# Recurrent mixer of a three-block layer stack: products on the two halves of the array's rows issued in turns

## The chip, the core and the metric

The kernel runs on one core of one Trainium2 chip. A core has a matrix engine (TensorE; PE in the profile, its weight loads PEld), a vector engine (DVE), a scalar engine (ACT), GpSimd (POOL) and a queue that issues transfers (SP). The matrix engine writes into PSUM, which has eight banks of 512 float32 numbers on each of 128 partitions. The metric is the device time of one execution in microseconds; lower is better.

## What is computed

Three transformer-like blocks run one after another on 1024 tokens of 1024 channels, all in float32. Only the second one matters here; of it, the recurrent group (eight heads of 64 channels). In short:

```python
def second_block(x, ...):
    h = rmsnorm(x, norm_mix_g[l])
    p = h @ w_in[l]
    p_rwkv = token_shift_mix(p[..., :D_RWKV_IN])
    y_rwkv = rwkv7_group(p_rwkv, ...)          # a state of 64x64 per head, carried over the tokens
    y_conv = conformer_conv_group(p[..., D_RWKV_IN:], ...)
    x = x + jnp.concatenate([y_rwkv, y_conv], axis=-1) @ w_out[l]
    ...                                         # feed-forward, norm
```

`rwkv7_group` updates a state per head at every token (a decay, a rank-one correction along a normalized key, and a new key-value product) and reads it with the receptance. The kernel computes it chunk by chunk: within a chunk of 64 tokens by products of matrices, from chunk to chunk by the state.

## The kernel before

The first and the third block, and the second block's projections and feed-forward, are long rows of matrix products from one helper (line 251). Between the second block's projections and its output projection stands the stage that the change touches: `rwkv`, lines 1242 to 1602.

It works on eight blocks of 128 tokens, two chunks of 64 in each, all eight heads at a time. A chunk's keys and directions lie on one half of the 128 partitions or the other, in such a way that what belongs to chunk 0 of a block and what belongs to chunk 1 meet on opposite halves. Many products therefore contract over 64 partitions alone (the upper or the lower half of the array's rows). For each block five generators run side by side, each on another block: `rwkv_prep` (the chunk's operands and their products within the chunk), `rwkv_solve` (small triangular inverses, on DVE and by transfers), `rwkv_pre` (what does not wait for the state), `rwkv_chain` (the state's way) and `rwkv_out` (norm and gate). `rwkv` puts them into rounds: in one round block i is in the chain, i + 1 in pre, i + 2 in solve, i + 3 in prep, i - 1 in out.

The six groups of products of 64 rows are these. For each the first operand is the half's weights, and each group wrote one PSUM bank and was read by one instruction before the next one of its kind:

- line 1336 in `rwkv_prep` (64 rows, 128 columns): four products for the decay from partitions 0 to 63, then four for the in-context rate from 64 to 127; each is followed by four tanh on ACT (line 1339).
- line 1403 in `rwkv_prep` (64 rows, 128 columns): the products of keys and directions with receptances, four times four, each four on one half; each is read by a masking product on DVE (line 1405).
- line 1465 in `rwkv_pre` (64 rows, 64 columns): eight products of one chunk, then eight of the other, each read by a masking product on DVE (line 1466).
- line 1480 (64 rows, 64 columns): eight products of chunk 0 after the first of three steps of a fixed-point iteration (line 1473, read at line 1475 on DVE), eight of chunk 1 after its second step; read by ACT (line 1481).
- lines 1488 and 1493 (64 rows, 64 columns): for chunk 0 eight and eight, then for chunk 1 eight and eight; read by ACT (lines 1489 and 1494). At line 1488 the output goes in turns to the upper and the lower 64 partitions, that is, to the two halves of the array's columns.

The banks have names with rounds of their own: `s` (prep) has two banks, `t` (pre) three. Each float32 product is carried out as two passes, so a product is two weight loads and two matmuls in the trace. After some steps of the generators (counted by their yields) a product for nothing stands on a third bank (`keep`, line 172), so that the matrix engine does not fall idle; its place among the matrix engine's instructions is fixed.

All other instructions are set in an order by a scheduler that runs while the kernel is built. It goes by the order in which the code lists them, by what each waits for, and by its own costs. It may move a product past others, so the order on the engine is not that of the code.

## Time and profile before

| | us |
|---|---|
| median of 3 runs | 3983.67 |
| fastest, slowest run | 3976.47, 3992.80 |
| span of the profiled execution | 3985.3 |
| matrix engine busy in it | 3836.2 (96%) |
| the recurrent stage with the first products of the output projection | about 380 (1123 to 1503) |

The profiled execution's own time is not recorded beside its span. The span is 1.6 us above the median of the runs, so what lies around the span cannot be told apart from the spread of the runs.

How to read the views: a PE row's duration is that of one instruction from issue to its end, and instructions overlap, so the pace is read from the starts. PEclk is the clock that the matrix engine was granted, as a share of 2.4 GHz; it has two levels, 1.00 and 0.50. A wait is put down to what came last.

### The profile page before, as it was taken

The page shows a single profiled execution, that of the slowest core. Times are in us where ns is not written, and L with a number is a line of the kernel's source. Part 1 is how long each engine was busy: PE and PEld are TensorE (multiplying, and loading weights), DVE is VectorE, ACT ScalarE, POOL GpSimd, SP SyncE. Part 2 cuts the span into 40 slices and gives each one's busy share as a digit, 9 for nine tenths or more (in the row PEclk, how much of TensorE's full clock was granted, in tenths as well). Part 3 has the DMA queues.
Part 4 walks back from the last instruction along what each step waited for, and adds up shares of the span by engine and source line. Part 5 has one row for each costly group of instructions (what it writes and reads, how often), then busy time and mean ns, then how long its engine had stood idle before and what let it go on. Part 6 is the DMA issues. An engine that isn't in the chain of part 4 may idle for free.

```text
span 3985.3 us, 57578 instructions
## 1 busy us (share of the span) xinstructions
PE 3836.2 (96%) x22592; PEld 3287.1 (82%) x22592; DVE 2131.0 (53%) x4925; ACT 1243.3 (31%) x2589; POOL 539.5 (14%) x825
## 2 busy tenths in 40 slices
PE   7999999799979989999999999999999999999998
PEld 6788888797868879888888898878899888888897
DVE  5356479668987865544444654444423444433154
ACT  4444436442232434222212232333422111121232
POOL 1011124300043410000000011111201211210000
PEclk9999999799977889999999999999999999999999
DMA  5321342431221233111111132112133222211143
GB/s 147 121 65 51 84 140 73 135 112 55 94 58 38 47 92 120 48 53 43 53 43 53 59 120 59 45 48 59 50 109 92 62 63 60 74 48 48 54 154 121
DMA packets 341697, 304.07 MB, mean 76 GB/s; under 512 B 51182, under 2 KB 305970, under 8 KB 341426
## 3 DMA queue, kind: packets, MB, share of 16 engines
q1 hardware_dynamic: 341426, 300.39, 24.3%
q8 instruction: 178, 2.92, 0.3%
q14 instruction: 93, 0.76, 0.1%
HBM read 234.27 MB, written 61.34 MB: 74 GB/s over the span
## 4 chain that ended last, share of the span: by engine, by line
PE 62%; DVE 2%; DMA 2%; ACT 1%; issue 1%; SPq 0%; POOL 0%; DVEq 0%; ACTq 0%; POOLq 0%
PE mm L251 54%; PE s L1798 2%; PE s L1972 1%; PE o L1820 1%; PE o L1872 1%; PE t L1865 0%; DMA wraw<-in_w_in_dram 0%; PE t L1897 0%; PE t L1842 0%; PE t L213 0%; DVE wlo L184 0%; PE o L1520 0%; PE f L172 0%; DMA alo<-ybT 0%; PE t L1465 0%
## 5 line engine op out<-in xcount | busy, mean ns | idle before, releaser
L251 PE MATMUL mm<-ahi,whi 128*128 128x512 f32 x2464 | 967.1, 394 | 0.5 <-ACT ahi L216 0.5
L251 PE MATMUL mm<-alo,whi 128*128 128x512 f32 x2464 | 965.3, 392 | 0.0
L251 PE MATMUL mm<-ahi,wlo 128*128 128x512 f32 x2464 | 963.4, 391 | 0.3 <-DVE wlo L184 0.3
L251 PE MATMUL mm<-whi,ahi 128*128 128x256 f32 (+2 forms) x1856 | 538.6, 291 | 16.4 <-ACT ahi L1612 7.5
L251 PEld LDWEIGHTS mm<-ahi,whi 128*128 128x128 f32 x2464 | 465.3, 189 | 96.9 <-ACT ahi L216 0.9
L251 PEld LDWEIGHTS mm<-ahi,wlo 128*128 128x128 f32 x2464 | 464.1, 188 | 97.0 <-DVE wlo L184 1.1
L251 PEld LDWEIGHTS mm<-alo,whi 128*128 128x128 f32 x2464 | 464.6, 189 | 94.1 <-issue 0.4
L183 ACT ACTIVATE whi<-wraw 128x1024 fp32r<-128x1024 f32 (+2 forms) x300 | 302.8, 1055 | 765.5 <-DMA wraw<-in_w_ff_dram 318.0
L251 PE MATMUL mm<-wlo,ahi 128*128 128x256 f32 (+2 forms) x1856 | 537.2, 290 | 1.8 <-DVE wlo L184 1.7
L251 PE MATMUL mm<-whi,alo 128*128 128x256 f32 (+2 forms) x1856 | 533.6, 289 | 2.0 <-DVE alo L218 1.5
L184 DVE TENSOR_TENSOR wlo<-wraw,whi 128x1024 fp32r<-128x1024 f32 (+2 forms) x300 | 357.5, 1229 | 332.6 <-PE mm L251 322.4
L251 PEld LDWEIGHTS mm<-whi,ahi 128*128 128x128 f32 x1856 | 358.2, 193 | 24.7 <-ACT ahi L1612 7.9
L251 PEld LDWEIGHTS mm<-wlo,ahi 128*128 128x128 f32 x1856 | 359.2, 194 | 7.6 <-issue 3.8
L251 PEld LDWEIGHTS mm<-whi,alo 128*128 128x128 f32 x1856 | 357.1, 193 | 6.1 <-issue 2.5
L1678 DVE TENSOR_TENSOR xm<-xm,mm 128x512 f32<-128x512 f32 x256 | 173.9, 686 | 120.1 <-PE mm L251 119.9
L251 PE MATMUL mm<-whi,ah 128*128 128x512 f32 x512 | 202.3, 395 | 0.0
L251 PE MATMUL mm<-wlo,ah 128*128 128x512 f32 x512 | 202.1, 395 | 0.0
L251 PE MATMUL mm<-whi,al 128*128 128x512 f32 x512 | 202.1, 395 | 0.0
L1170 DVE SCALAR_TENSOR_TENSOR cva<-cvh,vecs,cva 128x1022 f32<-128x1022 f32 (+29 forms) x120 | 145.4, 1263 | 0.2
L1660 DVE TENSOR_TENSOR fr<-fr 128x512 f32<-128x512 f32 x64 | 44.2, 690 | 154.1 <-ACT fr L1659 154.1
L207 POOL TENSOR_SCALAR x<-x,rT 128x1024 f32<-128x1024 f32 x16 | 18.8, 1174 | 760.9 <-PE mm L251 673.2
L251 PEld LDWEIGHTS mm<-whi,al 128*128 128x128 f32 x512 | 96.5, 188 | 22.5
(577 smaller groups left out, 5786.2 us busy)
## 6 DMA issues: line engine op xcount, KB each, us to landing
wraw<-in_w_in_dram SPq DMA_DIRECT2D x41, 1024.0 KB
wraw<-in_w_ff_dram SPq DMA_DIRECT2D x32, 1024.0 KB
wraw<-in_w_in_dram SPq DMA_DIRECT2D x59, 512.0 KB
wraw<-in_w_out_dram SPq DMA_DIRECT2D x24, 1024.0 KB
gv<-go SPq DMA_DIRECT2D x64, 128.0 KB
vl<-gv SPq DMA_DIRECT2D x16, 512.0 KB
wraw<-in_w_proj_a_dram SPq DMA_DIRECT2D x8, 1024.0 KB
wraw<-in_w_proj_b_dram SPq DMA_DIRECT2D x8, 1024.0 KB
```

The lines of the kernel that those rows point to most:

```text
L183: nc.scalar.activation(hi, src, AF.Copy)
L184: nc.vector.tensor_tensor(lo, src, hi.bitcast(F32), op=OP.subtract)
L207: nc.gpsimd.tensor_scalar(xn, xt, rs, 1.0, op0=OP.mult, op1=OP.mult)
L251: nc.tensor.matmul(out, lhs[a][:, kl, ls], rhs[b][:, kr, rs], start=first and n == 0, stop=last and n == tot - 1)
L1170: nc.vector.scalar_tensor_tensor(a[:, 30 - j:], h[:, 0:994 + j], wj, a[:, 30 - j:], op0=OP.mult, op1=OP.add)
L1660: nc.vector.tensor_tensor(r, r, r, op=OP.mult)
L1678: nc.vector.tensor_tensor(xm[t][:, ns], xm[t][:, ns], q, op=OP.add)
L1798: nc.tensor.matmul(q[:, :256], qk[:, a, qcol], qk[:, b, kcol], start=n == 0, stop=n == 2)
L1820: nc.tensor.matmul(ob[:, 128 * (b % 4):128 * (b % 4 + i1 - i0)], vt[:w, cc + 1], pt[:, 128 * i0:128 * i1], start=b % 4 == 0 and cc == b - ...
L1872: nc.tensor.matmul(o[:, 256 * (r % 2):256 * (r % 2) + 256], vg[:, r, kb], pt[:, 256 * kb:256 * kb + 256], start=kb == 0, stop=kb == 1)
L1972: nc.tensor.matmul(q[:, 128 * t:128 * t + 128], vl[:, 4 * hf + t], wt, start=True, stop=True)
```

## The change

Wherever two groups of products work on opposite halves of the array's rows, they are now listed in turns, a product of the one and a product of the other, and the two groups take two banks at once. The readers follow both. Nothing is added or removed: the products, their readers and the transfers are the same in number and size, and so are the places of the products for nothing, counted in yields.

Since the two chunks must now be listed together, two things move in `rwkv_pre`. The second chunk's group of line 1480 stands after the first step of the iteration, no longer after the second. And line 1488 of both chunks comes ahead of line 1493 of both. The diff, cut to its core (the rest removes comments):

```diff
-        for x, rows, b in ((sg, slice(0, 64), "w0"), (a, slice(64, 128), "a0")):
-            q = c.psum("s")
-            for pr in range(4):
-                ps = slice(128 * pr, 128 * pr + 128)
+        half = [slice(0, 64), slice(64, 128)]
+        qq = [c.psum("s") for _ in half]
+        for pr in range(4):
+            ps = slice(128 * pr, 128 * pr + 128)
+            for q, rows in zip(qq, half):
                 nc.tensor.matmul(q[:, ps], self.wup[rows, 0, ps], self.lwa[rows, js], start=True, stop=True)
+        for x, q, b in ((sg, qq[0], "w0"), (a, qq[1], "a0")):
...
-            for s in range(2):
-                rs = slice(64 * s, 64 * s + 64)
-                q = c.psum("s")
-                for pr in range(4):
+            qq = [c.psum("s") for _ in half]
+            for pr in range(4):
+                for q, rs in zip(qq, half):
                     nc.tensor.matmul(q[:, 128 * pr:128 * pr + 128], kb[rs, pr, 2 * b:2 * b + 2], va[rs, pr, 1 + 4 * b:3 + 4 * b],
                                      start=True, stop=True)
+            for s, q in enumerate(qq):
                 TT(gs[:, b, s:8:2], r4(q), m, op=OP.mult)
                 yield
...
-        for b in range(2):
-            ca = slice(64 * b, 64 * b + 64)
-            q = c.psum("t")
-            for h in range(8):
-                nc.tensor.matmul(q[Bh(b), H(h)], gs[Bh(b), b, h, ca], T16[Bh(b), h], start=True, stop=True)
+        qq = [c.psum("t") for _ in range(2)]
+        for h in range(8):
+            for b, q in enumerate(qq):
+                nc.tensor.matmul(q[Bh(b), H(h)], gs[Bh(b), b, h, 64 * b:64 * b + 64], T16[Bh(b), h], start=True, stop=True)
+        for b, q in enumerate(qq):
             TT(ET[Bh(b), :, Bh(b)], h8(q[Bh(b)]), self.mLow[Bh(b)].unsqueeze(1).to_broadcast([64, 8, 64]), op=OP.mult)
             yield
...
-            if i < 2:
-                q = c.psum("t")
+            if i == 0:
+                qq = [c.psum("t") for _ in range(2)]
                 for h in range(8):
-                    nc.tensor.matmul(q[Bh(i), H(h)], gs[Kh(i), i, h, Kh(i)], VU[i][Kh(i), H(h)], start=True, stop=True)
-                nc.scalar.activation(x1[Bh(i)], q[Bh(i)], AF.Copy)
-                yield
+                    for b, q in enumerate(qq):
+                        nc.tensor.matmul(q[Bh(b), H(h)], gs[Kh(b), b, h, Kh(b)], VU[b][Kh(b), H(h)], start=True, stop=True)
+                for b, q in enumerate(qq):
+                    nc.scalar.activation(x1[Bh(b)], q[Bh(b)], AF.Copy)
+                    yield
...
-        for b in range(2):
-            q = c.psum("t")
-            for h in range(8):
-                pr, s = h // 2, h % 2
+        qq = [c.psum("t") for _ in range(2)]
+        for h in range(8):
+            pr, s = h // 2, h % 2
+            for b, q in enumerate(qq):
                 nc.tensor.matmul(q[H(s), H(pr)], VU[b][Bh(b), H(h)], cur[Bh(b), H(h)], start=True, stop=True)
+        for b, q in enumerate(qq):
             nc.scalar.activation(va[:, :, 3 + b], q[:, 0:256].rearrange("p (r t) -> p r t", r=4), AF.Copy)
             yield
-            q = c.psum("t")
-            for h in range(8):
+        qq = [c.psum("t") for _ in range(2)]
+        for h in range(8):
+            for b, q in enumerate(qq):
                 nc.tensor.matmul(q[Bh(b), H(h)], cur[Bh(b), H(h)], x1[Bh(b), H(h)], start=True, stop=True)
+        for b, q in enumerate(qq):
             nc.scalar.activation((X if j or b else VU[b])[Bh(b)], q[Bh(b)], AF.Copy)
             yield
```

The scheduler sets the order anew, and it keeps the turns in some places only. In the order of the matrix engine's instructions, names with numbers are tiles: `t_...` and `s_...` are banks, `f_...` the bank of the products for nothing. Lines move by 2 to 9 in the changed file: 1336, 1403, 1465, 1473, 1480, 1488 and 1493 become 1338, 1405, 1468, 1477, 1485, 1494 and 1501.

First place: the matrix engine, lines 1465 and 1403 in one of the middle rounds, before:

```order
L1465 MATMUL t_2502_13163<-tp_2297_11699,gs_2191_11283 64x64 x8
L1465 MATMUL t_2507_13200<-tp_2297_11699,gs_2191_11283 64x64 x4
L172 LDWEIGHTS reset_11268
L172 MATMUL f_2500_13147<-reset_11268 128x384
L1465 MATMUL t_2507_13200<-tp_2297_11699,gs_2191_11283 64x64 x4
L1393 MATMUL s_2539_13455<-ws_2193_11285,blkR_11246 128x128 x4
L172 LDWEIGHTS reset_11268
L172 MATMUL f_2503_13173<-reset_11268 128x384
L1520 MATMUL o_2514_13230<-Sbd_11292,va_2189_11281 128x128 x4
L1403 MATMUL s_2542_13473<-va_2188_11280,kb_2192_11284 128x128 x4
```

The same place in the changed kernel, where each further pair of line 1468 reads like the first:

```order
L1468 MATMUL t_2502_13163<-tp_2297_11699,gs_2191_11283 64x64
L1468 MATMUL t_2503_13164<-tp_2297_11699,gs_2191_11283 64x64
...
L1405 MATMUL s_2542_13473<-va_2188_11280,kb_2192_11284 128x128
L1405 MATMUL s_2543_13474<-va_2188_11280,kb_2192_11284 128x128
L172 LDWEIGHTS reset_11268
L172 MATMUL f_2504_13182<-reset_11268 128x384
```

The two runs of eight have become pairs, and the second half's product of line 1405 now stands right behind the first half's. In the next round the same line 1468 stands in two runs again.

Second place: the matrix engine between the second and the third step of the iteration (line 1473), before:

```order
L1473 MATMUL t_2525_13304<-Pc_2517_13257,ws_2196_11288 64x64 x16
L172 LDWEIGHTS reset_11268
L172 MATMUL f_2527_13323<-reset_11268 128x384
L1568 MATMUL mm_2528_13334<-ident_72,O_2419_12622 128x128 x4
L1480 MATMUL t_2529_13344<-ws_2194_11286,gs_2191_11283 64x64 x8
L1403 MATMUL s_2544_13485<-va_2188_11280,kb_2192_11284 128x128
L1403 MATMUL s_2545_13491<-va_2188_11280,kb_2192_11284 128x128 x4
L1473 MATMUL t_2531_13366<-Pc_2526_13321,ws_2196_11288 64x64 x16
```

And in the changed kernel:

```order
L1477 MATMUL t_2528_13335<-Pc_2517_13257,ws_2196_11288 64x64 x10
L1405 MATMUL s_2544_13485<-va_2188_11280,kb_2192_11284 128x128
L1405 MATMUL s_2545_13486<-va_2188_11280,kb_2192_11284 128x128
...
L1585 MATMUL mm_2537_13438<-lora_9869,wup_11276 128x128 x4
L1477 MATMUL t_2531_13366<-Pc_2529_13352,ws_2196_11288 64x64 x16
L172 LDWEIGHTS reset_11268
L172 MATMUL f_2533_13385<-reset_11268 128x384
```

The eight products of line 1480 are gone from between the two steps, and line 1405 in turns and line 1585 fill the place.

Third place: the matrix engine, lines 1488 and 1493 of that block, before:

```order
L1488 MATMUL t_2535_13392<-Pc_2532_13383,ws_2194_11286 64x64 x8
L1493 MATMUL t_2536_13407<-X1_2501_13162,Pc_2532_13383 64x64 x8
L1488 MATMUL t_2538_13445<-Pc_2532_13383,ws_2194_11286 64x64 x8
L1367 MATMUL s_2587_13733<-ws_2193_11285,toh_11244 8x128 x4
L1493 MATMUL t_2540_13461<-X1_2501_13162,Pc_2532_13383 64x64 x8
```

And in the changed kernel, where again the further pairs of line 1494 read like the first:

```order
L1494 MATMUL t_2535_13392<-Pc_2532_13383,ws_2194_11286 64x64
L1494 MATMUL t_2536_13393<-Pc_2532_13383,ws_2194_11286 64x64
...
L1501 MATMUL t_2538_13445<-X1_2501_13162,Pc_2532_13383 64x64 x8
L172 LDWEIGHTS reset_11268
L172 MATMUL f_2546_13497<-reset_11268 128x384
L1370 MATMUL s_2588_13742<-ws_2193_11285,toh_11244 8x128 x4
L1501 MATMUL t_2539_13446<-X1_2501_13162,Pc_2532_13383 64x64 x8
```

Line 1494 is in turns; line 1501 has stayed in two runs of eight, with a product for nothing between them.

## Rows read from the trace of the kernel before

**Rows 1.** The page: busy time of the engines, and the granted clock in 40 slices.

```profile
PE 3836.2 (96%) x22592; PEld 3287.1 (82%) x22592; DVE 2131.0 (53%) x4925; ACT 1243.3 (31%) x2589; POOL 539.5 (14%) x825
PEclk9999999799977889999999999999999999999999
```

**Rows 2.** Windows: start:end, length, busy us per engine (instructions), then clock, DMA.

```profile
1217.00:1225.00 8.00, 8.00 (x119) 7.03 (x119) 5.56 (x14) 5.33 (x17) 3.19 (x4) 1.00 0.18 27
1200.00:1400.00 200.00, 190.21 (x2247) 163.63 (x2247) 165.79 (x390) 67.73 (x156) 72.67 (x101) 0.81 0.20 45
1123.00:1503.00 380.00, 329.28 (x3540) 283.04 (x3539) 287.79 (x708) 140.27 (x310) 132.62 (x172) 0.80 0.23 60
```

**Rows 3.** Waits of DVE, 1200 to 1400: us in total, times, longest.

```profile
DVE gs L1405 <- PE s L1403: 6.9, 6, 2.9
...
DVE Tc L1534 <- PE mm L1528: 0.8, 2, 0.6
```

**Rows 4.** Timeline of weight loads, 1216.5 to 1225: start, us, engine, line, tiles, count.

```profile
1217.64 0.19 PEld L1403 LDWEIGHTS s<-va,kb 64*128 64x128 f32 x1
1217.75 0.19 PEld L1336 LDWEIGHTS s<-lora,wup 64*128 64x128 f32 x1
1217.75 0.19 PEld L1403 LDWEIGHTS s<-va,kb 64*128 64x128 f32 x1
1217.86 0.64 PEld L1336 LDWEIGHTS s<-lora,wup 64*128 64x128 f32 x5
1218.62 0.54 PEld L1488 LDWEIGHTS t<-Pc,ws 64*64 64x64 f32 x16
...
1219.85 0.19 PEld L1488 LDWEIGHTS t<-Pc,ws 64*64 64x64 f32 x3
1219.90 0.14 PEld L1493 LDWEIGHTS t<-X,Pc 64*64 64x64 f32 x1
1219.91 0.18 PEld L1488 LDWEIGHTS t<-Pc,ws 64*64 64x64 f32 x2
1219.96 0.14 PEld L1493 LDWEIGHTS t<-X,Pc 64*64 64x64 f32 x1
...
1220.46 0.96 PEld L1336 LDWEIGHTS s<-lora,wup 64*128 64x128 f32 x8
...
1222.51 1.00 PEld L1493 LDWEIGHTS t<-X,Pc 64*64 64x64 f32 x16 [0.22 <-issue]
```

**Rows 5.** Line 1403 by itself: durations, and line 1405, its reader.

```profile
L1403 PEld LDWEIGHTS s<-va,kb x256: 182/188/334, 1141.6 to 1395.2; 64*128 64x128 f32 x128
...
L1405 DVE TENSOR_TENSOR gs<-s,mG x32: 671/681/693, 1143.4 to 1396.8; 128x512 f32<-128x512 f32 x32
```

**Rows 6.** Groups by line, 1123 to 1503, weight loads: count, busy us, mean ns, idle before.

```profile
L1403 PEld LDWEIGHTS s<-va,kb 64*128 64x128 f32 x256 | 32.6, 226 | 4.6 <-issue 1.7 <-DVE gs L1405 1.1 <-PE t L1227 0.6
L1465 PEld LDWEIGHTS t<-tp,gs 64*64 64x64 f32 x256 | 20.4, 169 | 3.3 <-issue 2.6 <-ACT ws L1458 0.2
L1480 PEld LDWEIGHTS t<-ws,gs 64*64 64x64 f32 x256 | 20.3, 164 | 4.3 <-DVE ws L1466 2.2 <-issue 1.2 <-PE t L1473 0.5
L1336 PEld LDWEIGHTS s<-lora,wup 64*128 64x128 f32 x128 | 16.2, 217 | 2.1 <-issue 0.8 <-DVE s L1215 0.3 <-DVE lnx L1221 0.3
```

**Rows 7.** Waits of the weight loads for nothing that the profile shows, 1123 to 1503.

```profile
PEld t L1465 <- issue: 2.6, 9, 0.7
...
PEld s L1367 <- issue: 0.3, 2, 0.2
```

**Rows 8.** Windows of 5 us from 1341, columns as in rows 2.

```profile
1341.00:1346.00 5.00, 4.94 (x40) 4.18 (x39) 4.70 (x10) 0.59 (x1) 1.76 (x2) 0.50 0.35 105
...
1351.00:1356.00 5.00, 5.00 (x66) 4.12 (x67) 3.33 (x10) 0.63 (x1) 0.00 (x0) 0.75 0.15 44
1356.00:1361.00 5.00, 5.00 (x84) 4.21 (x78) 4.64 (x14) 1.97 (x5) 0.64 (x1) 1.00 0.08 8
```

**Rows 9.** Timeline of PE, 1340 to 1354, columns as in rows 4.

```profile
1344.32 1.96 PE L1480 MATMUL t<-ws,gs 64*64 64x64 f32 x16
```

## The prediction

> **What bounds the kernel now.** The page comes first. PE is busy 96% of the span, and its clock stands at its full level in nearly all slices but a handful in the second quarter [rows 1]. Those slices are the recurrent stage, the only place that the change touches. So the question is what this stage can give.
>
> The windows by stage come next. From 1123 to 1503, 380 us, the granted clock is 0.80 on average [rows 2]. Its levels are 1.00 and 0.50, so PE ran at the lower one, 1.2 GHz, for (1.00 - 0.80) / 0.50 = 40% of it, some 152 us. In the middle, 1200 to 1400, PE is busy 190.2 us of 200 and DVE 165.8 [rows 2]. PE idled 9.8 us there. DVE waited for PE seven kinds of times in this stretch, from 6.9 us (line 1405 for line 1403) down to 0.8, 17.4 us together [rows 3]. So neither engine alone is the bound: they run in lockstep, and PE is the later one in 17.4 / (17.4 + 9.8) = 64% of the time in which one stands for the other. I take 0.6 as the share of any PE time saved or lost here that the end sees. It is a choice; 0 and 1 are its ends.
>
> Third, the timeline gives the pace of the products that change. All of it is read between 1217 and 1225, where the clock was 1.00 [rows 2]. The pace is from start to start: the length of a run less one load, over its count less one.
> - 64 rows by 128 columns, in one half: line 1336, (0.96 - 0.19) / 7 = 0.110 us a pass [rows 4].
> - The same shape in turns: lines 1403 and 1336 happen to stand in turns at 1217.64 to 1217.86, and two loads start every 0.11 us, 0.055 a pass [rows 4].
> - 64 rows by 64 columns in one place: line 1493, (1.00 - 0.14) / 15 = 0.057 [rows 4].
> - Line 1488, whose output alternates between the column halves within one row half: (0.54 - 0.14) / 15 = 0.027 [rows 4]. It has half the pace already.
> - Lines 1488 and 1493 mixed, three places of the array in play: six loads start from 1219.85 up to 1219.96, 0.018 a pass [rows 4].
>
> **What the change gives, step by step.** It gives only where turns really stand in the new order. I counted in the order of PE's instructions the products that follow one of the same line on the other bank. Line 1403: 15 of 128 before, 51 after. Line 1336: 5 of 64, then 16. Line 1465: 4 of 128, then 44. Line 1480: none, then 14. Line 1493: none, then 2. Line 1488: none, then 120 of 128. So the scheduler undoes most turns but those of line 1488, which needs them least.
>
> A product is two passes, so turns save one pass's 0.110 or 0.057 us per product at the full clock. Part of the time the clock is low: line 1403's loads take 188 ns at the median, 334 at most [rows 5], 226 in the mean [rows 6], so (226 - 188) / (334 - 188) = 26% of them were slow. I use 1.26 for all but line 1488.
> - Lines 1403 and 1336: (36 + 11) x 0.110 x 1.26 = 6.5 us.
> - Lines 1465, 1480 and 1493: (40 + 14 + 2) x 0.057 x 1.26 = 4.0 us.
> - Line 1488: 120 x 2 passes x (0.027 - 0.018) = 2.2 us. The row with three places is the nearest; the low end is nothing, since the pace of four places is not in the trace.
>
> Together 12.7 us of PE time, 10.5 without line 1488.
>
> The Trainium skill, page "TensorE: Matmul & The Clock Gate", section "Part 3: Packing small matmuls — row/col tiling", says that a weight load overlaps a running matmul only if it goes to another row group. By that rule line 1488 would gain most, 120 x 2 x (0.057 - 0.027) = 7.2 us instead of 2.2. The row does not bear it out: within one row half it already ran at 0.027 [rows 4].
>
> **What it costs.** *Banks.* Lines 1403 and 1336 have two banks and now take both at once. The first product of the next pair waits until one reader is done, the second until both are. Behind that wait PE's whole queue stands, the iteration of line 1473 among it. Line 1403's loads waited 1.1 us for this reader in the whole stage [rows 6]; a reader takes 0.68 us [rows 5]. Bounds: nothing, since other products stand between most pairs in the new order, and one further reader for each of 16 pairs, 10.9 us. A gain is excluded, since no bank comes free earlier than now. I take 2 us, the nearer row doubled.
>
> *Changes of shape.* Loads stand still for nothing that the profile shows, about 0.2 to 0.3 us at a time, where the next product has another shape than the last: 2.6 us in 9 times at line 1465 [rows 7]. Eleven such groups, from 2.6 us down to 0.3 at line 1367, make 16.3 us. Neighbours of different shape number 236 in the stage's order before and 269 after, counted line by line. So 16.3 / 236 = 0.07 us each, and 33 more of them cost 2.3 us. The bounds are nothing and 33 x 0.29 = 9.6.
>
> The Trainium skill, page "TensorEngine Tiling", section "Key Properties", says that a change of the tiling mode drains the engine. By that each of the 33 would pay the full 0.29, 9.6 us, and eat most of the gain. The rows agree that there is such a stop [rows 7], but show it at a third of the changes at most.
>
> *Moves.* The second chunk's group of line 1480 leaves the place between the second and third steps of the iteration, where it gave PE work while DVE made the next operand (line 1475). In the new order line 1405 and line 1585 stand there, so I cost it at nothing; without that cover it would be about one reader's 0.68 us per block, 5 us. Line 1489's ACT copy comes half a group later and line 1493's follow together; ACT is busy 67.7 of 200 us [rows 2], so nothing. The transfers of SP and POOL's work are the same. In the third block a few instructions at the end of the attention swap places; as many as before, so nothing.
>
> **The sum.** 12.7 - 2.0 - 2.3 = 8.4 us of PE time, 0.6 of it at the end: 5.0 us. The profiled span of 3985.3 becomes 3980.3. The median of the runs is 1.6 us under that span, so I forecast **3979 us**. With all costs low and the whole gain seen it is 3984 - 13 = 3971, with all costs high (12.7 - 10.9 - 9.6 = -8) 3992. The runs before differ from their median by up to 9 us, so this case's own range is 3964 to 3998.
>
> **Rivals.** *The clock returns sooner (faster).* From 1341 to 1346 PE was busy 4.94 us of 5 and yet at 0.50; the clock came back within the window from 1351 and was full from 1356 on [rows 8]. In that stretch stood runs on half the array such as line 1480's, 1.96 us for 16 passes [rows 9]. Were they through in half the time, the dense products behind them would come sooner. If the low stretches shrink by a third, 50 us go from half to full speed, 25 us of PE time, 15 at the end with 0.6: 3979 - 15 = 3964, and 3954 if all is seen. Against it: most turns of those lines are undone, and DVE holds the stage too. I say 3960, chance 0.20.
>
> *The clock falls once more (slower).* Shorter runs leave PE waiting for DVE more often, and in the iteration the product for nothing that followed its second step (between the two line 1473 runs) is gone from there. 152 us in about ten stretches are 15 us each; one more costs 15 x 0.5 x 0.6 = 4.6 us at the end. One more just cancels the forecast; from six on the kernel is slower by over 20 us. With six: 3979 + 27 = 4006. For it: the lockstep, in which PE waits if it is early. Against it: total work stays, and other products fill the place. Chance 0.16.
>
> *The change does not do what it says.* The two halves' products in turns save nothing, or bank waits and shape changes cost what they save: 3984. The turns at 1217.64 speak against the first [rows 4]. Chance 0.14.
>
> **How the numbers follow.** The forecast has 0.50. A measurement of this kernel tells about 0.5%, 20 us, from no change. The forecast and the third rival lie within that: 0.64. Faster by more: 0.20, slower by more: 0.16. The range for 8 in 10 takes in the own range of the likeliest case and reaches into both clock rivals: 3959 to 4003.
>
> **What would show each step.** Right: outside 1123 to 1503 all stages as long as before; lines 1468 and 1405 at about half the pace where they stand in turns; line 1494 at 0.018 to 0.027 a pass; waits of line 1405's loads for line 1407 of some 3 us; the clock of the stage near 0.80. Wrong: a stage clock under 0.75 or over 0.87 (a clock rival), loads in turns still 0.057 or 0.110 apart, or PE standing over 10 us for line 1407.

## The result

The changed kernel takes 3964.84 us (median of 7 runs, 3956.31 to 3971.84). The kernel before took 3988.27 us beside it (7 runs, 3976.47 to 3998.59). The ratio is 0.9946, with a 95% interval of 0.9936 to 0.9957: about 21 us, half a per cent. The forecast was 3979, its range 3959 to 4003. The range held the time, but the gain is four times the 5 us of the sum: the time came out where the rival of a clock that returns sooner had it (3964).

The profiled execution took 3971.84 us, its span is 3970.0. The page of the changed kernel, beside [rows 1]:

```profile
PE 3815.7 (96%) x22592; PEld 3267.0 (82%) x22592; DVE 2124.3 (54%) x4925; ACT 1243.0 (31%) x2589; POOL 538.9 (14%) x825
PEclk9999998799978989999999999999999999999999
```

As many products as before, 20.5 us less of them. Two digits of the clock in the second quarter are higher, one ahead of it is lower. The windows (start:end, length, busy us per engine with instructions, clock, DMA) say the same, beside [rows 2]:

```profile
1123.00:1503.00 380.00, 325.80 (x3689) 279.17 (x3688) 293.66 (x723) 145.90 (x316) 132.35 (x172) 0.85 0.27 74
1200.00:1400.00 200.00, 184.74 (x2414) 155.72 (x2413) 176.92 (x442) 75.24 (x170) 77.06 (x106) 0.91 0.22 51
```

The clock of the stage went from 0.80 to 0.85. With levels of 0.50 and 1.00 that is 30% of 380 us at the lower level, 114 us instead of 152. In the middle it went from 0.81 to 0.91.

The stage now ends earlier, so a fixed window holds more of what comes after it. From here on the stage is cut from the first product of line 1212 to the last product of the gate in `rwkv_out` (line 1576 before, 1585 after). It then holds the same 3507 weight loads in every kernel, and 3508 or 3509 matmuls (in e8 3501, where seven of line 172 were not recorded). Before:

```profile
1125.00:1497.00 372.00, 322.11 (x3509) 276.57 (x3507) 284.83 (x705) 140.11 (x310) 132.62 (x172) 0.80 0.23 59
```

After:

```profile
1127.40:1478.80 351.40, 299.17 (x3508) 253.90 (x3507) 279.72 (x705) 139.57 (x310) 132.35 (x172) 0.85 0.24 63
```

The stage is 20.6 us shorter: the whole gain lies in it. What stands ahead of it came out 2.4 us longer in this one execution, what stands behind it 2.9. PE is busy 22.9 us less and idle 52.2 us instead of 49.9. DVE does the same work in 5.1 us less. Its waits for PE, all rows of the stage added, fell from 40.6 to 23.6 us, while those for ACT rose from 13.9 to 23.7 and PE's own for DVE from 32.3 to 37.2. In the middle, 1200 to 1400, the waits of DVE (total, times, longest) were 17.4 us for PE [rows 3] and are now 6.4:

```profile
DVE Pc L1479 <- PE t L1477: 2.8, 3, 1.1
DVE gs L1408 <- PE s L1405: 2.3, 2, 2.2
...
DVE ws L1531 <- PE o L1529: 0.8, 2, 0.5
...
DVE n L1372 <- PE s L1370: 0.3, 1, 0.3
...
DVE Tc L1543 <- PE mm L1537: 0.2, 1, 0.2
```

The weight loads by line in the stage after (count, busy us, mean ns, idle before), beside [rows 6]. Lines 1403, 1465, 1480, 1336, 1488 and 1493 are now 1405, 1468, 1485, 1338, 1494 and 1501:

```profile
L1405 PEld LDWEIGHTS s<-va,kb 64*128 64x128 f32 x256 | 25.7, 212 | 5.0 <-issue 1.5 <-DVE gs L1408 0.8 <-DVE kb L1391 0.8
L1485 PEld LDWEIGHTS t<-ws,gs 64*64 64x64 f32 x256 | 20.2, 166 | 3.6 <-issue 1.2 <-DVE ws L1470 1.0 <-DVE ws L1433 0.2
L1468 PEld LDWEIGHTS t<-tp,gs 64*64 64x64 f32 x256 | 16.3, 155 | 2.4 <-issue 1.5 <-ACT ws L1374 0.3
L1501 PEld LDWEIGHTS t<-X,Pc 64*64 64x64 f32 x256 | 15.9, 135 | 3.6 <-ACT va L1496 2.8 <-ACT X L1503 0.2 <-ACT ws L1342 0.2
L1338 PEld LDWEIGHTS s<-lora,wup 64*128 64x128 f32 x128 | 14.8, 215 | 3.0 <-issue 1.2 <-DVE gs L1408 1.1 <-DVE ws L1433 0.3
L172 PEld LDWEIGHTS <-reset 128*128 128x128 bf16 x88 | 8.3, 98 | 7.0 <-issue 1.1
L1494 PEld LDWEIGHTS t<-Pc,ws 64*64 64x64 f32 x256 | 4.5, 134 | 2.6 <-DVE Pc L1479 1.9 <-issue 0.3 <-ACT ws L1342 0.2
```

The three of these lines of before that do not stand in [rows 6]:

```profile
L1493 PEld LDWEIGHTS t<-X,Pc 64*64 64x64 f32 x256 | 16.2, 135 | 1.2 <-issue 0.6 <-ACT X L1494 0.4
L172 PEld LDWEIGHTS <-reset 128*128 128x128 bf16 x88 | 8.8, 102 | 6.6 <-issue 1.4
L1488 PEld LDWEIGHTS t<-Pc,ws 64*64 64x64 f32 x256 | 8.7, 134 | 2.8 <-DVE Pc L1475 2.1
```

The six changed lines went from 114.4 to 97.4 us, 17.0 less. Line 172, the product for nothing, is one gauge of the clock's part: its work is the same in both, and its loads went from 8.8 to 8.3 us, 6% less. Six per cent of 114.4 are 6.5 us, so some 10.5 us are left to the turns. It is a rough gauge, since it stands at other moments than the six lines: by their own mean loads (line 1403 from 226 to 212 ns, 1465 from 169 to 155, 1336 from 217 to 215, 1480 from 164 to 166, the two others unchanged) the clock's part is 3.6 us, and 13.4 are left. The sum had 12.7.

The trace has the granted clock of every stretch, so the same can be counted for the whole stage. PE was busy 120.6 us at the lower clock before and 79.9 after. If a busy us at the lower clock is counted at half, PE's work in the stage is 261.8 us at full speed before and 259.2 after, 2.6 less. Counted by what a single load of line 1403 lengthens (188 to 334 ns, 1.78 times), it is 5.1 less. So, by this estimate, of the 22.9 us of busy time that went, 18 to 20 went with the clock and 3 to 5 with everything else, turns and costs together.

How the clock falls and returns can be read in one place of the changed kernel. The timeline of PE (start, us, what, idle before it):

```profile
1329.31 0.83 PE L1396 MATMUL s<-ws,blkR 128*128 128x128 f32 x6
1333.58 2.04 PE L1529 MATMUL o<-Sbd,va 128*128 128x128 f32 x8 [3.44 <-DVE ws L1433]
```

And the windows of 5 us around it:

```profile
1322.00:1327.00 5.00, 5.00 (x62) 4.22 (x60) 4.75 (x10) 3.31 (x6) 2.96 (x5) 1.00 0.20 20
1327.00:1332.00 5.00, 3.14 (x32) 2.54 (x31) 4.78 (x9) 0.63 (x1) 3.00 (x3) 0.98 0.19 56
1332.00:1337.00 5.00, 3.42 (x20) 3.13 (x20) 4.83 (x10) 0.00 (x0) 0.72 (x2) 0.50 0.16 49
1337.00:1342.00 5.00, 5.00 (x55) 4.27 (x54) 3.66 (x11) 0.61 (x2) 1.40 (x4) 0.50 0.19 56
1342.00:1347.00 5.00, 5.00 (x65) 4.17 (x65) 2.48 (x8) 1.78 (x4) 0.62 (x1) 0.66 0.00 0
1347.00:1352.00 5.00, 4.64 (x75) 3.86 (x71) 4.72 (x13) 1.92 (x5) 1.30 (x1) 1.00 0.02 4
```

PE stood 3.44 us for DVE, up to 1333.58, and by then its clock had gone to 1.2 GHz. From there it was busy without a gap up to 1347 (3.42, 5.00 and 5.00 us of the three windows), yet at 0.50 up to 1342 and, by the mean of 0.66, for two thirds of the next window. One wait of 3.4 us is followed by over 11 us of work at half speed.

### The profile page after: what moved, and what is told of

Read it like the earlier page. It is cut to its first block, busy times and chain, and to the rows that moved or that the text cites. A ratio compares the mean times of both kernels' runs of the same rounds, so it can differ in the third digit from the quotient of the medians.

```text
span 3970.0 us, 57579 instructions
## 1 busy us (share of the span) xinstructions
PE 3815.7 (96%) x22592; PEld 3267.0 (82%) x22592; DVE 2124.3 (54%) x4925; ACT 1243.0 (31%) x2589; POOL 538.9 (14%) x825
## 3 DMA queue, kind: packets, MB, share of 16 engines
q1 hardware_dynamic: 341426, 300.39, 24.6%
## 4 chain that ended last, share of the span: by engine, by line
PE 62%; DVE 2%; DMA 1%; ACT 1%; issue 0%; SPq 0%; POOL 0%; DVEq 0%; ACTq 0%; POOLq 0%
PE mm L251 55%; PE s L1807 2%; PE o L1829 1%; PE s L1981 1%; PE o L1881 1%; DMA wraw<-in_w_in_dram 0%; PE t L1874 0%; PE t L1851 0%; PE t L1906 0%; PE t L213 0%; DMA catT<-y 0%; DVE wlo L184 0%; PE t L1477 0%; DMA alo<-ybT 0%; PE o L1548 0%
## 5 line engine op out<-in xcount | busy, mean ns | idle before, releaser
L251 PEld LDWEIGHTS mm<-whi,ahi 128*128 128x128 f32 x1856 | 358.9, 194 | 22.9 <-ACT ahi L1621 7.4
L1813 POOL TENSOR_SCALAR mS<-mS,s 128x256 f32<-128x256 f32 x128 | 60.9, 478 | 399.0 <-DVE s L1812 339.9
```

The costliest lines, as they stand in the source:

```text
L251: nc.tensor.matmul(out, lhs[a][:, kl, ls], rhs[b][:, kr, rs], start=first and n == 0, stop=last and n == tot - 1)
L1813: nc.gpsimd.tensor_scalar(S_, S_, r, 1.0, op0=OP.mult, op1=OP.mult)
```

## The experiments

Three theories were to be told apart. The first is that of the rival "the clock returns sooner": the turns shorten products, and most of the gain is a clock that stays up. The second: the turns' pace alone brings it. The third: the two banks, the moves, or chance in the scheduler's new order bring it.

No edit changes one thing alone, since the scheduler sets the whole stage anew for each. How far an order has moved can be counted in the traces: the least number of DVE's 705 instructions in the stage that must change place to turn one kernel's order into the other's. From the kernel before it is 228 to the changed kernel, 209 to 324 to e1, e2, e3, e4, e6 to e11, 121 to e12, and only 37 to e5.

All kernels and the results in one table. "In turns" counts products that follow one of the same line on the other bank, at lines 1336 (of 64) and 1403 (of 128), then at 1465, 1480, 1488 and 1493 together (of 512). Clock is the mean granted clock over the span, averaged over the runs. Stage, PE busy in it and DVE's waits for PE in it come from the one profiled execution of each, which need not be a middling one: the changed kernel's was the longest of its 7 (3971.84 us), e4's the shortest of its 6 (3955.35).

| kernel | in turns | median us (runs) | ratio to before, 95% | clock | stage us | PE busy | DVE waits for PE |
|---|---|---|---|---|---|---|---|
| before | 5, 15, 4 | 3983.95, 3986.83, 3985.84 (21, 28, 23) | | 0.9677 | 372.0 | 322.1 | 40.6 |
| changed | 16, 51, 180 | 3964.84 (7) | 0.9946 [0.9936, 0.9957] | 0.9729 | 351.4 | 299.2 | 23.6 |
| e1, all six in runs | 27 of 640 in all | 3977.12 (12) | 0.9978 [0.9966, 0.9991] | 0.9701 | 365.7 | 326.8 | 40.7 |
| e2, 1336 and 1403 | 18, 43, 4 | 3967.20 (6) | 0.9944 [0.9927, 0.9961] | 0.9748 | 353.7 | 295.8 | 29.9 |
| e3, the other four | 4, 12, 188 | 3975.86 (10) | 0.9973 [0.9959, 0.9987] | 0.9703 | 367.5 | 317.7 | 43.2 |
| e4, all pinned | 54, 107, 457 | 3960.49 (6) | 0.9930 [0.9914, 0.9947] | 0.9732 | 347.4 | 275.6 | 23.9 |
| e5, 1336 and 1403 in runs | 5, 15, 4 | 3987.50 (12) | 1.0004 [0.9993, 1.0016] | 0.9678 | 369.1 | 317.3 | 44.8 |
| e6, 1403 alone | 4, 47, 6 | 3978.18 (12) | 0.9983 [0.9972, 0.9994] | 0.9714 | 361.6 | 307.5 | 28.0 |
| e7, e4 with 128 columns | 53, 105, 461 | 3975.30 (10) | 0.9972 [0.9963, 0.9982] | 0.9692 | 361.9 | 280.7 | 32.9 |
| e8, e4 with 512 columns | 54, 106, 456 | 3968.92 (5) | 0.9959 [0.9947, 0.9970] | 0.9750 | 356.5 | 272.1 | 25.4 |
| e9, line 1480 moved | 5, 13, 4 | 3991.72 (11) | 1.0010 [0.9999, 1.0021] | 0.9682 | 376.4 | 330.5 | 47.4 |
| e10, e11 with the moves | 52, 106, 14 | 3966.01 (5) | 0.9951 [0.9938, 0.9964] | 0.9726 | 353.3 | 292.4 | 47.0 |
| e11, 1336 and 1403 pinned | 48, 106, 5 | 3987.92 (12) | 1.0007 [0.9998, 1.0017] | 0.9700 | 380.6 | 316.7 | 54.7 |
| e12, 1336 alone | 21, 14, 5 | 3971.92 (5) | 0.9967 [0.9955, 0.9979] | 0.9702 | 360.2 | 311.5 | 37.8 |

The runs of the kernel before, taken beside the experiments, say something on the clock by themselves. Its order is the same each time, but its clock is not: 5 runs at 0.965 took 3990.8 us in the mean, 19 at 0.967 took 3986.5, 11 at 0.969 took 3983.5, 6 at 0.971 took 3979.9. Over its 72 runs the time goes by 2.0 us for each 0.001 of clock (correlation -0.83). Over all kernels here, each taken around its own mean, it is 2.27. As 0.001 of 3985 us are 4.0 us of TensorE at full speed, the end sees 2.27 / 4.0 = 0.57 of it. That is another reading of the share that the prediction chose as 0.6, though not of this stage alone: the clock is that of the whole span, and it is low elsewhere too (0.96 ahead of the stage in the profiled execution). It is also a correlation: a run that waits more could have the lower clock for it.

**e1: all six places listed as in the change, but in runs.**

```diff
-            for pr in range(4):
-                for s, q in enumerate(qq):
+            for s, q in enumerate(qq):
+                for pr in range(4):
```
(and likewise with h and b at the other places)

> The changed kernel with its listing, its two banks at once and its moves, but each group in a run again (no turns). Turns between halves in the order: 27 of 640, against 24 before and 247 with the change. If the gain of 21.5 us comes from the turns, by their pace or by a clock that returns sooner: 3978 to 3996, low-clock time of the stage near 150 us. If it comes from the moves or from the order that the scheduler happens to make: 3960 to 3976.

Measured: 3977.12, ratio 0.9978 [0.9966, 0.9991], between the two expectations. Without any turns added the new listing is about 9 us faster, less than half of the change's gain. Its clock is up by 0.0024, which by the slope is 5.4 us of it. So a part of the gain does not need the turns; the rest does, or needs another order.

**e2: turns at lines 1336 and 1403 alone, and e3: at the four others alone.** Each undoes one part of the change. Line 1403 in e2 (line 1336 likewise), and line 1465 in e3 (likewise lines 1480, 1488 and 1493):

```diff
-            for s in range(2):
-                rs = slice(64 * s, 64 * s + 64)
-                q = c.psum("s")
-                for pr in range(4):
+            qq = [c.psum("s") for _ in range(2)]
+            for pr in range(4):
+                for s, q in enumerate(qq):
+                    rs = slice(64 * s, 64 * s + 64)
...
```

```diff
-        for b in range(2):
-            ca = slice(64 * b, 64 * b + 64)
-            q = c.psum("t")
-            for h in range(8):
+        qq = [c.psum("t") for _ in range(2)]
+        for h in range(8):
+            for b, q in enumerate(qq):
...
```

> Turns at lines 1336 and 1403 alone, the rest as before (18 of 64 and 43 of 128 in turns). By the forecast's sum these lines give 6.5 of 12.7 us of PE time, so about half of the whole gain: 3977 (3970 to 3984). If the clock is what counts: any gain goes with the low-clock time, 4 us less of it for each us of time. If the order's luck decides: no relation to the share, 3960 to 3995.

> Turns and moves at lines 1465, 1480, 1488 and 1493 alone (44, 21, 120 and 3 of 128 in turns), lines 1336 and 1403 as before. By the forecast's sum the other half of the gain: 3978 (3970 to 3985). If the moves do it: as fast as the changed kernel, 3965.

Measured: e2 3967.20 (0.9944), the whole gain of the change, where the sum had half of it; e3 3975.86 (0.9973), about 11 us, as expected, but hardly more than e1 gave with no turns. The two gains do not add: by the ratios 22 and 11 us apart, 21 together. So the listing of the preparation alone, lines 1336 and 1403, comes with the whole gain. It is not their pace that shows in the stage: counted as above, PE's work in e2 is 0.7 us more than before or 2.7 less, while its busy time at the lower clock fell from 120.6 to 66.6 us. The 120 turns of line 1488, the only place that the scheduler left as written, brought nothing that a measurement here can tell: e3 and e1 are 1.3 us apart.

**e4: the change with its turns pinned.** The scheduler undoes most turns; here it must keep them.

```diff
-                    nc.tensor.matmul(q[:, 128 * pr:128 * pr + 128], ...
+                    ins = nc.tensor.matmul(q[:, 128 * pr:128 * pr + 128], ...
+                    if not (q is qq[0] and pr == 0):
+                        c.tc.keep_in_program_order(ins)
...
```

> The changed kernel, with each product of a pair of groups pinned behind the one listed ahead of it, so that 618 of 640 stand in turns (247 with the change). PE time freed by the forecast's rows: 141 x 0.139 + 333 x 0.072 + 3 = 47 us, 0.6 of it at the end: 3988 - 28 + 3 = 3963 by pace alone if the order costs nothing, under 3950 if the clock stays up as well. If the turns do nothing and the order was luck: 3960 to 4000, low-clock time no shorter than 113 us.

Measured: 3960.49, ratio 0.9930 [0.9914, 0.9947]. Of all kernels it has the lowest time, near the 3963 that was expected by pace alone, but its interval overlaps that of the change, so it is not told apart from it. PE's busy time in the stage is 46.5 us under that of before and 23.6 under that of the change. Its stage:

```profile
1118.60:1466.00 347.40, 275.61 (x3508) 228.10 (x3507) 283.01 (x705) 138.35 (x310) 134.17 (x172) 0.86 0.25 63
```

PE idles 71.8 us of it, before 49.9. Beside the changed kernel, 23.6 us less of busy time gave a stage shorter by 4.0 us. DVE is busy 283.0 us and waits for PE no less (23.9) than in the changed kernel, while PE's own waits grew: for DVE from 37.2 to 48.4 us, for ACT from 10.4 to 17.5. So in this pair of executions, past the point that the change reaches, faster products mostly wait longer for the others. Two executions 16 us apart in all bear this, so it is a hint and no measure.

**e5: lines 1336 and 1403 with two banks, but in runs.** The partner of e2; the diff is from e2 to it, and likewise at line 1336.

```diff
-            for pr in range(4):
-                for s, q in enumerate(qq):
+            for s, q in enumerate(qq):
+                for pr in range(4):
...
```

> The products of lines 1336 and 1403 listed with their two banks as in the changed kernel, but each half in one run, no turns (5 of 64 and 15 of 128 stand in turns, as before); the other places as before. Theory 1, that the turns bring the gain (shorter products, and a clock that comes back sooner for it): as the kernel before, 3984 us within 5, mean clock 0.968. Rival, that the two banks and the other order of issue bring it: 3967, as with turns at these two lines, mean clock 0.974.

Measured: 3987.50, ratio 1.0004 [0.9993, 1.0016]. Two banks taken at once cost and give nothing here; the order is also nearly that of before (37 of 705). Between e5 and e2 only the turns in the listing differ, and with them the order that the scheduler makes of it, in which 219 of DVE's 705 instructions change place: 20 us. Which of the two brings them is not separated.

**e6 and e12: turns at line 1403 alone, at line 1336 alone.** e6 has the edit of e2 without the one at line 1336, e12 has that one alone, shown here:

```diff
-        for x, rows, b in ((sg, slice(0, 64), "w0"), (a, slice(64, 128), "a0")):
-            q = c.psum("s")
-            for pr in range(4):
-                ps = slice(128 * pr, 128 * pr + 128)
+        half = [slice(0, 64), slice(64, 128)]
+        qq = [c.psum("s") for _ in half]
+        for pr in range(4):
+            ps = slice(128 * pr, 128 * pr + 128)
+            for q, rows in zip(qq, half):
...
```

> Turns at line 1403 alone (47 of 128 stand in turns, 15 before), line 1336 and all others as before. Theory 1: the gain goes with the number of turns, and line 1403 has two thirds of those added at the two places, so two thirds of 17 us: 3972, clock 0.972. Rival, that line 1336, the first step of the preparation, brings it since all else follows it: 3984, clock 0.968.

> Turns at line 1336 alone (21 of 64, 4 before). Theory 1: what line 1403 alone did not give of the 19 us of both together is given here: 3975 within 4, clock 0.971. Rival, that neither alone gives much and the two together passed a point at which the clock stays up: 3984.

Measured: 3978.18 (0.9983) and 3971.92 (0.9967). They do add up to e2: 7 and 13 us by the means, 20 together. But not by the count of turns. Line 1336 has 16 turns more than before, worth 16 x 0.110 x 1.26 = 2.2 us of TensorE time, and brought 13. So the products' pace is not the size of the gain. e12's clock gives 5.7 us by the slope; where the other 7 lie is not shown. Neither of the two expectations had the sizes right: line 1403 has most turns, and line 1336 the larger gain.

**e7 and e8: the products for nothing of e4 at 128 and at 512 columns instead of 384.** They were meant to test the clock by itself. The turns stay (618, then 619 and 616), but the order does not: from e4 to e7 at least 233 of DVE's 705 instructions in the stage change place, to e8 232, as many as from the kernel before to the changed one.

```diff
-FN = 384
+FN = 128
```
(e8: `FN = 512`)

> The listing with nearly all turns pinned, and the 88 products for nothing that the kernel issues in this stage cut from 384 columns to 128: by the trace one lasts 0.33 us at full clock and would last 0.11, so 19 us of TensorE time less. Theory 1, that the granted clock is what the rest of the gain goes by, and that it follows how busy TensorE is: mean clock falls under 0.968, and with 2.27 us for each 0.001 (the slope within runs of one order) the time is 3960 + 12 - 11 = 3961 or more, up to 3985. Rival, that the clock has nothing to do with it and TensorE's time alone counts: 3960 - 0.57 x 19 = 3950 at an unchanged clock of 0.973.

> The same listing with the 88 products for nothing at 512 columns: 10 us more of TensorE time. Theory 1: mean clock rises by 0.002 or more, and the time comes out at 3960 + 5.5 - 4.5 or more below = 3961 or lower, 3952 at best. Rival, that the clock has nothing to do with it: 3966 at clock 0.973.

Measured: 3975.30 at a clock of 0.9692, and 3968.92 at 0.9750, beside 3960.49 at 0.9732. The stage of e7:

```profile
1119.10:1481.00 361.90, 280.65 (x3508) 238.15 (x3507) 284.15 (x705) 140.03 (x310) 135.44 (x172) 0.82 0.23 61
```

The products for nothing (count, busy us, mean ns, idle before) in e4, then in e7:

```profile
L172 PE MATMUL f<-reset 128*128 128x384 bf16 x88 | 31.1, 353 | 0.1
L172 PE MATMUL f<-reset 128*128 128x128 bf16 x88 | 21.4, 243 | 0.1
```

So 9.7 us of TensorE work are gone, not the 19 that the expectation worked out by columns, and the stage is 14.5 us longer. PE's busy time even grew by 5.0 us, since more of it ran at 1.2 GHz: 102.9 us, against 72.4 in e4. The rival that the clock is nothing and work is all had 3950 and does not fit; the clock stayed above the 0.968 that theory 1 had named. But whether the shorter products for nothing lowered the clock, or the new order did, is not separated. And more is not better: e8 has the higher clock and is 8.4 us slower, where 3961 or less was expected. Its products for nothing last 401 ns in the mean, 48 more, which is 4.2 us of added work for 88 and not 10; with the 4 us that the clock should have given back, some 12 us were lost, more than all of it. The new order may have cost them; that is not shown.

These two also show the limit of the slope. From e4 to e7 it gives 9.1 us for the clock, and 9.7 us less work should have given some back, yet the kernel lost 14.8. So a split of a gain into a clock's part and the rest, by that slope, is an estimate to within some 10 us between orders.

**e9: one move alone.** The second chunk's products of line 1480 and its copy come one step earlier, nothing else.

```diff
-            if i < 2:
-                q = c.psum("t")
-                for h in range(8):
-                    nc.tensor.matmul(q[Bh(i), H(h)], gs[Kh(i), i, h, Kh(i)], ...
+            if i == 0:
+                qq = [c.psum("t") for _ in range(2)]
+                for b, q in enumerate(qq):
+                    for h in range(8):
+                        nc.tensor.matmul(q[Bh(b), H(h)], gs[Kh(b), b, h, Kh(b)], ...
...
```

> The kernel before with one move alone: the second half's products of line 1480 (and their copy out of PSUM) one step earlier, beside the first half's, in two runs and two banks. Theory 1, that the 9 us that the two-banks-in-runs kernel gained comes of this move: 3976, mean clock 0.970. Rival, that it comes of line 1488's two halves ahead of line 1493's, or of chance in the order: 3986, clock 0.968.

Measured: 3991.72, ratio 1.0010 [0.9999, 1.0021]. The 9 us of e1 are not this move's. With e5 that leaves the listing of lines 1465, 1488 and 1493 in two banks, the interplay of all, or chance in the order; it was not taken further apart.

**e11: turns pinned at lines 1336 and 1403 alone, and e10: the same with the four other places listed as in the change, in runs.** From e2 to e11 (line 1403; line 1336 likewise); e10 has beside it the edit of e1 at the other places.

```diff
-                    nc.tensor.matmul(q[:, 128 * pr:128 * pr + 128], ...
+                    ins = nc.tensor.matmul(q[:, 128 * pr:128 * pr + 128], ...
+                    if not (q is qq[0] and pr == 0):
+                        c.tc.keep_in_program_order(ins)
```

> Turns pinned at lines 1336 and 1403 alone (48 of 64, 106 of 128; 18 and 43 where they were not pinned), all others as before. By the paces 93 more turns at 0.138 us are 13 us of TensorE time; with 0.57 of it seen 7 us below 3967: 3960, and lower still if the clock rises above 0.975. Rival, that VectorE bounds the stage by then: 3967 as without the pins.

> Turns pinned at lines 1336 and 1403 (52 of 64, 106 of 128), and the four other places listed with two banks and the moves, but in runs. Beside the next kernel it shows what the moves give once the preparation is in turns, and beside the one with all turns pinned (3960) what turns at the four places give. Theory 1, that the gains do not add because VectorE and the chain take over: 3960 within 4, all three alike. Rival, that they add: moves give 9 us more than the next kernel, and turns at the four places of this one's products another 8 us or more below it, so that this one is at 3968.

Measured: e11 3987.92 (1.0007 [0.9998, 1.0017]), e10 3966.01 (0.9951 [0.9938, 0.9964]). This is the largest miss of the study. e11 has over twice the turns of e2 at the same two lines, and all of e2's gain is gone: its stage clock is 0.82, that of e2 0.87. Both expectations for e11 fell. e10's time is near the 3968 of its rival, but by luck: that had it 9 us below e11, and it is 22. The stage of e11:

```profile
1124.40:1505.00 380.60, 316.70 (x3508) 266.54 (x3507) 281.80 (x705) 140.36 (x310) 135.59 (x172) 0.82 0.22 58
```

PE is busy 5.4 us less than in the kernel before and idle 63.9 us instead of 49.9. DVE's longest sums of waits in it:

```profile
DVE ws L1529 <- PE o L1527: 21.1, 6, 8.3
DVE gs L1412 <- PE s L1407: 12.6, 6, 3.5
```

Line 1527 (1520 before) is the state's product, a link of the chain from block to block; DVE waited 8.7 us for it in the kernel before, here 21.1. The longest of these waits, in the timeline:

```profile
1218.98 0.42 DVE L1523 TENSOR_TENSOR Sbd<-Tc,ff 64x256 f32<-64x256 f32 x1
...
1219.72 2.07 PE L1407 MATMUL s<-va,kb 64*128 64x128 f32 x14
...
1222.16 1.48 PE L1546 MATMUL o<-ws,gs 128*64 128x64 f32 x12
...
1223.67 0.59 ACT L1548 ACTIVATE O<-o 64x512 f32<-64x512 f32 x1 [4.78 <-PE o L1546]
...
1226.61 0.68 PE L1472 MATMUL t<-tp,gs 64*64 64x64 f32 x6 [1.37 <-DMA tp<-lane]
1227.21 2.07 PE L1337 MATMUL s<-lora,wup 64*128 64x128 f32 x14
...
1229.51 1.41 PE L1527 MATMUL o<-Sbd,va 128*128 128x128 f32 x8
...
1231.03 0.68 DVE L1529 TENSOR_TENSOR ws<-o,X 64x512 f32<-64x512 f32 x1 [8.32 <-PE o L1527]
```

The state that line 1527 reads was written by 1219.40, and its product began at 1229.51. The first half of this is a bank: `o` has one alone in this stage, and it came free at 1224.26, when ACT had copied what line 1546 left there. The last twelve passes of line 1546 stood behind the pinned group of line 1407. In the second half, 5.3 us, the rows show nothing that line 1527 still lacked; line 1337's pinned group, and even a group that waited 1.37 us for a DMA, stand ahead of it in PE's queue. A pin keeps a product behind the one listed ahead of it; that the pins made this order is likely and not shown. Nor is it shown that this is the whole of the difference between e11 and e10: e10 has the same pins, its DVE waits 9.2 us for that line, and 47.0 for PE in all.

## Why the prediction was right, and where it was not

The time lies in the range, at the lower end of the likeliest case's own (3964 to 3998). That is partly luck: the likeliest case had the clock unchanged, and by the estimates below the clock made half of the gain or more. The base was also low by some 2 us: the sum took 1.6 us off the span, while the changed kernel's profiled execution took 1.8 us more than its span, and the kernel before took 3985.8 us in the mean of 72 runs.

**The bound and the share of 0.6: fitting, as far as it can be read.** The slope of time on clock within one order gives 0.57, for the whole span. The waits of DVE for PE in the stage fell by 17.0 us of the 20.6 that it became shorter, so DVE does see what PE saves. From the kernel before to e4 the share is 24.6 / 46.5 = 0.53, but from the changed kernel to e4 4.0 / 23.6 = 0.17: the lockstep may have an end, which the one share did not say.

**The paces: right but for one.** In the changed kernel two runs in turns stand at the full clock (start, us):

```profile
1218.21 0.56 PEld L1494 LDWEIGHTS t<-Pc,ws 64*64 64x64 f32 x32 [0.17 <-issue]
...
1238.64 0.97 PEld L1405 LDWEIGHTS s<-va,kb 64*128 64x128 f32 x16 [0.17 <-DVE s L1562]
```

Line 1405: (0.97 - 0.19) / 15 = 0.052 us a pass, forecast 0.055. Line 1494: (0.56 - 0.14) / 31 = 0.0135, forecast 0.018, so its gain is 240 x (0.027 - 0.0135) = 3.2 us and not 2.2. The Trainium skill, page "TensorE: Matmul & The Clock Gate", section "Part 3: Packing small matmuls — row/col tiling", states the overlap of a load with running products only for another row group. The rows show both: columns in turn within one row half run at 0.027 a pass [rows 4], and the row halves in turn on top of it halve that again.

**The 12.7 us of TensorE time: about right for the six lines, not for the stage.** The gauges above leave 10.5 to 13.4 us. Line 1480 gave nothing (20.3 to 20.2 us, 1.0 forecast), line 1488 4.2 of loads (2.2 forecast), lines 1336 and 1403 gave 8.3 of loads, part of it clock, against 6.5. Less the costs, 8.4 us of TensorE time were to be free in the stage; counted by its clock it was 3 to 5.

**Banks, 2.0 us: somewhat high, well within the bounds.** The loads of line 1405 waited 0.8 us for the reader (line 1408; the prediction's signs call it 1407), and those of line 1338 another 1.1, against 1.1 before: under a microsecond more. e5 puts the two banks at 0 within some 5 us.

**Changes of shape, 2.3 us: it fits, but one pair of executions cannot bear it out.** The stops of the weight loads for nothing that the profile shows, all rows of the stage added, went from 27.4 us in 76 to 29.3 in 80, 1.9 more; in the other orders they lie between 23.0 (e2) and 42.2 (e8). The Trainium skill, page "TensorEngine Tiling", section "Key Properties", states that a change of tiling mode drains the engine. A stop of 0.29 us at each of the 33, 9.6 us in all, is not borne out by these rows.

**Moves, nothing: nearly.** ACT's copy, which I costed at nothing, is a new wait: line 1501's loads stood 2.8 us for line 1496 (group above). e9 puts the move of line 1480 at no gain.

**The clock: wrong, and this is the step that failed.** The likeliest case left it at 0.80, and the sum of 5.0 us came out of that. It rose to 0.85; 38 us of the stage changed from half to full speed, where the rival had 50. With the rival's own working that is 19 us of TensorE time and 11 at the end. The count above says the same of TensorE: 40.7 us less of its busy time stood at the lower clock. By the slope the mean clock, up from 0.9677 to 0.9729, gives 11.7 us of the 21.2 between the means. The other 9.5 us are 5.0 of pace and costs as summed, and 4.5 that no term had. Either estimate puts half of the gain on the clock, the largest single term. I gave this case 0.20 because the scheduler undoes most turns and DVE holds the stage. The first is no argument: e12, with 16 turns more at one early line and the order that came of them, was 13 us faster. The mark set for it, a stage clock over 0.87, was also too far off; 0.85 was enough for most of its price.

**What is shown and what is not.** Shown: the gain lies in the stage; the listing of lines 1336 and 1403 in turns comes with the whole of it, and in runs they give nothing (e2, e5); with the gain goes less busy time of TensorE at the lower clock, 40.7 us less in the changed kernel and 54.0 in e2. Not shown: why the clock stays up. It may be the shorter products, or the places that the scheduler gives them, and a stage with fewer waits could have the better clock for that. Orders with no turns added lie from 3977 to 3992 (e1, e5, e9), orders with them from 3960 to 3988. The same two lines in turns are worth 20 us in one order (e2) and nothing in another, with pins (e11). Three kernels with nearly the same turns lie 15 us apart as well (e4, e7, e8). So chance in the order stands as a rival that no run here excludes.

## What to carry to other kernels

Where two engines run in lockstep and TensorE's clock drops when it waits, price a change by what it does to the waits and the clock, and not by the pace of its products alone: here the clock was half of the gain by estimate, at 2.3 us for each 0.001 of its mean. The runs of the unchanged kernel already hint at this price (2.0 us), since their clock and their time vary together in one fixed order. Where a scheduler sets the order, a local edit moves much else: here three orders with no turns added lie 15 us apart, so a gain of 20 us needs other orders beside it before it is put down to the edit. And pinning an order can cost more than a faster pace gives, if a link of a chain comes to stand behind the pinned products: look there in the trace for a wait whose operand and whose bank were ready long before.

## What the runs showed of the hardware

Products of 64 rows by 64 columns on all four quarters of the array in turn started every 0.0135 us, a quarter of the 0.057 in one place, as if four ran side by side. In e4, line 1471 with its turns pinned shows the pace for two places:

```profile
1217.69 1.00 PEld L1471 LDWEIGHTS t<-tp,gs 64*64 64x64 f32 x30
```

(1.00 - 0.14) / 29 = 0.030 us a pass, half of 0.057.

Less work can go with more time: with 9.7 us of products for nothing taken out, and the order that came of it, the stage grew by 14.5 us and TensorE's busy time by 5.0. After one wait of 3.44 us TensorE was at 1.2 GHz for more than 11 us in which it was busy throughout.
